# Three DRAM-to-DRAM weight sums of a hybrid encoder layer at other places of the weight plan

## The chip, the cores and the metric

The kernel runs on one core of a Trainium2 chip. The metric is the device time of one execution in microseconds; the time given for a kernel is the median of its runs. A profile is one further execution, taken with the hardware profiler; its times count from the first instruction.

## What is computed

One layer over 512 tokens of width 1024: an S5 state-space branch and a gated-MLP branch are merged by gates, then comes attention to 256 memory tokens, then a SwiGLU feed-forward with an inner width of 2816. Cut to what matters here:

```python
def memory_cross_attention(hn, memn, w_q, w_k, w_v, w_o):
    q = (hn @ w_q).reshape(bsz, seq, XATTN_HEADS, XATTN_HEAD_DIM)
    k = (memn @ w_k).reshape(bsz, MEM_LEN, XATTN_HEADS, XATTN_HEAD_DIM)
    v = (memn @ w_v).reshape(bsz, MEM_LEN, XATTN_HEADS, XATTN_HEAD_DIM)
    ...
    return o @ w_o

def swiglu(hn, w_gate, w_up, w_down):
    return (jax.nn.silu(hn @ w_gate) * (hn @ w_up)) @ w_down

        h = h + memory_cross_attention(rms_norm(h, xattn_norm_g[i]), memn,
                                       w_q[i], w_k[i], w_v[i], w_xo[i])
        h = h + swiglu(rms_norm(h, ffn_norm_g[i]), w_gate[i], w_up[i], w_down[i])
```

## The kernel before

**Split products.** Every float32 operand is split into a rounded high half (`whi`, a cast on ScalarE, line 85) and the rest (`wlo`, a subtraction on VectorE, line 86). A product takes three matmuls: high by high, high by low, low by high (`mm3`, line 358).

**Seven products for eight.** The products with w_proj_b, w_q, w_gate, w_up and w_down are made by a Strassen-Winograd scheme: of each 2 x 2 split of the weights, seven products instead of eight, four of which (numbers 4 to 7) need sums of weight blocks. For w_proj_b, w_q and w_down these sums are made in DRAM, ahead of time, by transfers alone. For w_down the results are `dsum4` to `dsum7`, each cut into six chunks of 512 KB, the last of 256 KB. Sum 5 and sum 7 add two blocks of w_down; sum 6 adds a block to sum 5, sum 4 a block to sum 6.

**The plan.** All weights are listed once, in the order of their use, in `plan`: 218 entries, each one block of at most 512 KB. An entry has a list of loads and a function that makes its two halves. `next_w` (called where TensorE's program takes entry i) starts the loads that are due by then and makes the halves up to two entries ahead. A load into SBUF is due three entries ahead (`LOADS`) and has three buffers (`wraw`), so the load of an entry waits until the halves of the entry three before are made; the two kinds of halves have three buffers each too.

The entries around the change: 64 to 71 are w_k, 72 to 79 are w_v (two halves of four blocks, two token tiles each, so 12 matmuls for a block), 80 to 93 the fourteen products with w_q (six blocks of w_q itself and eight of its sums, `qsum`), 94 to 101 w_xo, and 102 to 107 the first blocks of w_gate and w_up: 102 and 104 are the last 256 gate columns, 103 and 105 the first two blocks of the first gate unit, 106 and 107 the last 256 up columns. From 108 on come the units of the feed-forward, seven products each, and at the end w_down.

**The sums' places.** `plan_sums` makes a list of 40 jobs, in this order: sixteen for w_proj_b and w_q, then six chunks each of `dsum5`, `dsum7`, `dsum6` and `dsum4`. A job is two transfers: a plain copy of the first block from DRAM to DRAM, issued by SP (line 274), and an accumulating copy that adds the second block to it, issued by POOL (GpSimd, line 275). Job number m gets the m-th place (j, step): its copy is issued when entry j is taken, its accumulation when entry j + step is taken. The accumulation waits for the copy's landing.

**Queues.** SP issues nearly all loads, in order, so that a waiting load holds up those behind it. POOL issues the accumulations, in order too, and computes the norm factors (`r`, line 497), which a row's scaling (`xs`, line 512, VectorE) and its transposes (`ptr`, line 520, TensorE) wait for. The order on each engine is fixed when the program is built, by a scheduler with a model of time; a few instructions, the plain copies of the sums among them, are kept in the program's order.

Of the kernel before, what the change touches and what calls it, by code (L numbers as in the profile page):

```python
# [52 lines left out]
def hybrid_layer_kernel(  # L53
# [203 lines left out]
    def plan_sums(places):  # L257


        jobs = []  # L260
        pairs = {5: ((0, 0), (0, 1)), 7: ((0, 1), (1, 1)), 6: (None, (1, 1)), 4: (None, (1, 0))}
        for w, sums, qs in ((w_proj_b, bsum, (5, 7, 6)), (w_q, qsum, (5,)), (w_proj_b, bsum, (4,)), (w_q, qsum, (7, 6, 4))):
            for q in qs:
                first, more = pairs[q]
                for n in range(2):
                    jobs.append((sums[q, n], sums[q + (-1 if q == 6 else 2), n] if first is None else
                                 pair_block(w, *first, n), pair_block(w, *more, n)))
        for q, i, jc, more in ((5, 0, 0, lambda c: down_block(0, 1, c)), (7, 0, 1, lambda c: down_block(1, 1, c)),
                               (6, 1, 1, lambda c: down_sum(5, c)), (4, 1, 0, lambda c: down_sum(6, c))):
            for c in range(CHUNKS):  # L270
                jobs.append((down_sum(q, c), down_block(i, jc, c), more(c)))
        assert len(jobs) == len(places)
        for (dst, src, more), (j, step) in zip(jobs, places):
            plan[j][1].append((0, lambda d=dst, x=src: tc.keep_in_program_order(nc.sync.dma_start(d, x))))
            plan[j + step][1].append((0, lambda d=dst, x=more: nc.gpsimd.dma_start(d, x, accum_op=ALU.add)))
# [41 lines left out]
    for i in range(4):  # L317
# [5 lines left out]
    plan_units(UNITS, down_plan)  # L323

    plan_sums([(5, 3), (7, 3), (9, 2), (13, 5), (14, 5), (16, 4)] + [(18 + 2 * i, 3) for i in range(8)] +
              [(51 + 2 * i, 2) for i in range(4)] + [(85 + 3 * i, 3) for i in range(3)] +
              [(95 + 2 * i, 2) for i in range(3)] + [(122 + 4 * i, 4) for i in range(16)])
    used_w = [0]

    def next_w(*key):  # L330
# [1515 lines left out]
```

## Time and profile before

| | |
|---|---|
| median of 3 runs | 881.05 us (880.0 to 881.38) |
| profiled execution | 883.48 us |
| its span, first to last instruction | 881.7 us |
| mean granted TensorE clock | 0.992 |
| copies into `dsum` by SP | 24 (20 of 512 KB, 4 of 256 KB) |
| accumulations into `dsum` by POOL | 24 |

How it is read: the page gives busy times by engine and the chain of waits that ended last; the windows give busy times and the share of the DMA engines in a stretch of the span; a row of the timeline has its start, its length, engine and line, what it writes from what, and in brackets how long the engine was idle before it and what ended that. A DMA's row on SP or POOL is its issue, not its transfer; the time to landing is listed with the DMA issues.

### The profile page before, as it was taken

Reading aid. Unit: us, or ns where it says so; the run is one execution under the profiler, and the core shown is the slowest. Engines: PE = TensorE matmul, PEld = TensorE weight load, DVE = VectorE, ACT = ScalarE, POOL = GpSimd, SP = SyncE. Lnnn points to the kernel's source line nnn. Section 1 sums busy time; section 2 is a strip of 40 time slices with the busy share of each in tenths; the row PEclk is TensorE's granted clock in tenths of the full one; section 3 lists DMA queues with packets and bytes.
Section 4 is the critical chain, followed back from the end, with each engine's and each line's share of the span. In section 5 each row is a group of like instructions: output and inputs, shape, how many; then the busy total and the mean of one; then the engine's idle time right before and its main releaser. Section 6 shows DMA issues by size and latency. Waiting matters only on the chain.

```text
span 881.7 us, 14747 instructions
## 1 busy us (share of the span) xinstructions
PE 863.3 (98%) x5760; PEld 769.7 (87%) x5760; DVE 658.4 (75%) x1068; ACT 467.2 (53%) x692; POOL 86.4 (10%) x117
## 2 busy tenths in 40 slices
PE   8999999999998999999999999999999999999996
PEld 5788888888888988889899878999999999988875
DVE  5699885899845777658856836767878767899875
ACT  5643953244366553547555535645455455656664
POOL 1001301311000001100001001101211111000010
PEclk8999999999999999999999999999999999999999
DMA  7769565898664798735679645647999998366672
GB/s 239 197 191 298 104 179 148 183 234 193 166 195 115 241 285 258 245 112 156 207 218 256 172 108 159 168 123 168 228 232 236 211 239 215 96 187 207 193 237 96
DMA packets 117256, 169.56 MB, mean 192 GB/s; under 512 B 9265, under 2 KB 82497, under 8 KB 117058
## 3 DMA queue, kind: packets, MB, share of 16 engines
q1 hardware_dynamic: 97602, 141.64, 50.6%
q0 software_dynamic: 19296, 26.45, 19.2%
q8 instruction: 45, 0.74, 0.3%
q10 hardware_dynamic: 288, 0.52, 0.2%
q14 instruction: 25, 0.20, 0.1%
HBM read 159.71 MB, written 48.73 MB: 236 GB/s over the span
## 4 chain that ended last, share of the span: by engine, by line
PE 91%; DMA 4%; ACT 2%; DVE 2%; SPq 1%; issue 1%; POOL 0%; POOLq 0%; ACTq 0%; DVEq 0%
PE pf L358 26%; PE pt L358 17%; PE px L1146 12%; PE pq L1146 6%; PE dx L358 5%; PE dq L358 3%; PE pv L1146 3%; PE bx L1146 2%; PE qx L1146 2%; PE dv L358 2%; PE pz L889 2%; PE ptr L520 1%; PE po L358 1%; PE qv L1146 1%; DMA slab<-in_s_log_step_dram 1%; DMA wraw<-qsum 1%
## 5 line engine op out<-in xcount | busy, mean ns | idle before, releaser
L85 ACT CAST whi<-wraw 128x1024 fp32r<-128x1024 f32 (+1 forms) x145 | 148.6, 1025 | 158.0 <-PE pf L358 48.6
L86 DVE TENSOR_TENSOR wlo<-wraw,whi 128x1024 fp32r<-128x1024 f32 (+1 forms) x145 | 171.9, 1188 | 69.1 <-ACT whi L85 67.4
L358 PE MATMUL pf<-xn,whi 128*128 128x512 f32 x448 | 140.4, 393 | 0.0
L358 PEld LDWEIGHTS pf<-xn,whi 128*128 128x128 f32 x448 | 83.7, 188 | 17.5 <-issue 0.4
L358 PE MATMUL pf<-xn,wlo 128*128 128x512 f32 x224 | 87.8, 392 | 0.0
L1146 PE MATMUL px<-fn,whi 128*128 128x256 f32 x480 | 83.3, 276 | 0.0
L1146 PEld LDWEIGHTS px<-fn,whi 128*128 128x128 f32 x480 | 72.6, 188 | 0.2
L86 DVE TENSOR_TENSOR wlo<-b,whi 128x1024 fp32r<-128x1024 f32 x40 | 48.9, 1222 | 27.9 <-ACT whi L85 27.9
L85 ACT CAST whi<-b 128x1024 fp32r<-128x1024 f32 x40 | 42.2, 1054 | 50.8 <-PE px L1146 27.8
L1146 PE MATMUL px<-fn,wlo 128*128 128x256 f32 x240 | 66.4, 277 | 0.0
L1146 PE MATMUL pq<-s,whi 128*128 128x256 f32 x320 | 55.0, 276 | 0.0
L358 PE MATMUL dx<-whi,s 128*128 128x512 f32 x170 | 53.4, 391 | 0.4 <-DVE h L1771 0.4
L86 DVE TENSOR_TENSOR wlo<-t,whi 128x1024 fp32r<-128x1024 f32 x30 | 36.7, 1224 | 19.4 <-ACT whi L85 19.4
L85 ACT CAST whi<-t 128x1024 fp32r<-128x1024 f32 x30 | 31.6, 1053 | 35.3 <-PE pv L1146 12.4
L358 PEld LDWEIGHTS pf<-xn,wlo 128*128 128x128 f32 x224 | 42.1, 188 | 8.7 <-issue 0.2
L1146 PEld LDWEIGHTS pq<-s,whi 128*128 128x128 f32 x320 | 48.2, 188 | 0.0
L358 PE MATMUL pt<-whi,xn 128*128 128x512 f32 x128 | 44.6, 415 | 1.6 <-ACT xn L85 1.4
L1146 PEld LDWEIGHTS px<-fn,wlo 128*128 128x128 f32 x240 | 45.1, 188 | 0.0
L1146 PE MATMUL pq<-s,wlo 128*128 128x256 f32 x160 | 44.2, 276 | 0.0
L358 PEld LDWEIGHTS dx<-whi,s 128*128 128x128 f32 x170 | 31.8, 188 | 7.5 <-issue 0.8
L358 PE MATMUL dx<-wlo,s 128*128 128x512 f32 x85 | 33.1, 391 | 0.3 <-DVE wlo L86 0.3
L358 PEld LDWEIGHTS pt<-whi,xn 128*128 128x128 f32 x128 | 24.7, 195 | 7.8 <-ACT xn L85 2.0
(451 smaller groups left out, 2200.7 us busy)
## 6 DMA issues: line engine op xcount, KB each, us to landing
wraw<-in_w_in_dram SPq DMA_DIRECT2D x36, 512.0 KB, 4.6
dsum<-in_w_down_dram SPq DMA_DIRECT2D x20, 512.0 KB, 5.7
wraw<-dsum SPq DMA_DIRECT2D x20, 512.0 KB, 3.8
b<-in_w_gate_dram SPq DMA_DIRECT2D x15, 512.0 KB, 6.6
b<-in_w_up_dram SPq DMA_DIRECT2D x15, 512.0 KB, 5.6
wraw<-in_w_down_dram SPq DMA_DIRECT2D x15, 512.0 KB, 4.5
dsum<-in_w_down_dram POOLq DMA_DIRECT2D x10, 512.0 KB, 7.8
dsum<-dsum POOLq DMA_DIRECT2D x10, 512.0 KB, 7.6
```

The costliest lines, as they stand in the source:

```text
L85: hi = nc.scalar.copy(dst_hi, src)
L86: lo = nc.vector.tensor_tensor(dst_lo, src, dst_hi.bitcast(F32), ALU.subtract)
L358: m = nc.tensor.matmul(ps, a[x], b[y], start=start and i == 0, stop=stop and i == 2, skip_group_check=free)
L520: nc.tensor.transpose(ps[:, j, :], src[:, k * P:(k + 1) * P], ident)
L889: nc.tensor.matmul(ps[:, g, :], wt[:, g, :], u[:, o * GO + g, :], start=True, stop=True)
L1146: nc.tensor.matmul(ps[:, j, :], a[x], b[y], start=start and j == k == i == 0, stop=k == 3 and i == 2, skip_group_check=True)
```

## The change

Only the list of places changes. The three places 85, 88 and 91 among w_q's entries go; 73 and 76 among w_v's entries come, and 105 among the first gate and up blocks. Since jobs take the places in order, the jobs after them slide:

| job | before | after |
|---|---|---|
| 18: sum 5, chunk 2 | entry 85, added at 88 | 73, added at 76 |
| 19: sum 5, chunk 3 | 88, 91 | 76, 79 |
| 20: sum 5, chunk 4 | 91, 94 | 95, 97 |
| 21: sum 5, chunk 5 (256 KB) | 95, 97 | 97, 99 |
| 22: sum 7, chunk 0 | 97, 99 | 99, 101 |
| 23: sum 7, chunk 1 | 99, 101 | 105, 108 |

```diff
     plan_sums([(5, 3), (7, 3), (9, 2), (13, 5), (14, 5), (16, 4)] + [(18 + 2 * i, 3) for i in range(8)] +
-              [(51 + 2 * i, 2) for i in range(4)] + [(85 + 3 * i, 3) for i in range(3)] +
-              [(95 + 2 * i, 2) for i in range(3)] + [(122 + 4 * i, 4) for i in range(16)])
+              [(51 + 2 * i, 2) for i in range(4)] + [(73, 3), (76, 3)] +
+              [(95 + 2 * i, 2) for i in range(3)] + [(105, 3)] + [(122 + 4 * i, 4) for i in range(16)])
```

In the built program SP's copy of job 18 stands between w_v's fourth and fifth load, that of job 19 between its seventh and eighth, that of job 23 behind the second `wraw` load of w_up and ahead of the first unit's up blocks. On POOL the accumulation of job 23 stands between the third and the fourth norm factor of the feed-forward's norm. The other engines have the same instructions in the same order.

## The prediction

> **What bounds the kernel now.** I read the page first: its span, the busy times and the shares of the chain that ended last.
>
> ```profile
> span 881.7 us, 14747 instructions
> PE 863.3 (98%) x5760; PEld 769.7 (87%) x5760; DVE 658.4 (75%) x1068; ACT 467.2 (53%) x692; POOL 86.4 (10%) x117
> PE 91%; DMA 4%; ACT 2%; DVE 2%; SPq 1%; issue 1%; POOL 0%; POOLq 0%; ACTq 0%; DVEq 0%
> ```
>
> TensorE is busy for 863.3 of 881.7 us, so a change in transfers is worth only the TensorE idle time that it removes or adds. Then came the chain of waits over w_q's products, where the three sums stood:
>
> ```profile
> 459.84 9.48 DMA wraw<-qsum
> ...
> 471.78 2.39 PE qq L1146 x18
> ```
>
> The chain shows a load of 9.48 us, but a step of a chain is not a loss: TensorE was working most of that time. The loss is TensorE's idle time, in the windows (stretch and its length, busy us and count of PE, PEld, DVE, ACT and POOL, the clock, the share of DMA, GB/s) and in the waits:
>
> ```profile
> 468.00:472.00 4.00, 3.62 (x32) 3.42 (x31) 1.50 (x2) 2.58 (x4) 1.14 (x1) 1.00 1.01 296
> sum 42.00, PE 41.40 PEld 40.36 DVE 27.87 ACT 25.50 POOL 4.31; mean PE 0.49 PEld 0.48 DVE 0.33 ACT 0.30 POOL 0.05
> PE qq L1146 <- DVE wlo L86: 0.4, 1, 0.4
> PE ppt L1432 <- DVE prob L1423: 0.2, 1, 0.2
> ```
>
> The sum is over 84 windows of half a microsecond from 449 to 491, the whole stretch after the first of the three copies: TensorE is idle for 42.00 - 41.40 = 0.60 us in all. Of that the late weights cost 4.00 - 3.62 = 0.38 us, once; the other 0.22 is the wait of the transposes (ppt) for the softmax, which holds no weight load.
>
> **The change, part by part.** TensorE, ScalarE and VectorE keep every instruction and its order; only the places of plain copies (SP, line 274) and accumulating copies (POOL, line 275) move. Jobs 18 and 19 (third and fourth chunk of sum 5) go from w_q's entries 85 and 88 to w_v's 73 and 76. The next four jobs slide one place down the list of places: 91, 95, 97, 99 become 95, 97, 99, 105. So entry 91 is freed and 105 is new. No copy and no byte is added: 24 copies and 24 accumulations stay.
>
> *Removed from w_q's products:* three copies and three accumulations. Beside them two loads took 7.3 and 9.5 us, where the median of w_v's (below) is 3.7 (DMA issues, each from a window with that issue alone, issued at 457.12 and 459.84):
>
> ```profile
> wraw<-qsum SPq DMA_DIRECT2D x1, 512.0 KB, 7.3
> wraw<-qsum SPq DMA_DIRECT2D x1, 512.0 KB, 9.5
> 455.68 1.18 POOL L275 DMA_DIRECT2D dsum<-in_w_down_dram  x1 [54.58 <-DMA dsum<-in_w_down_dram]
> 457.51 0.56 SPq L274 DMA_DIRECT2D dsum<-in_w_down_dram  x1
> 468.65 1.14 POOL L275 DMA_DIRECT2D dsum<-in_w_down_dram  x1 [11.79 <-DMA dsum<-in_w_down_dram]
> ```
>
> Worth: -0.38 us. Upper bound -0.60, if the softmax's 0.22 goes as well; lower bound 0, if the loads stay late. I take -0.4. What is late next there is the softmax's wait.
>
> *Added among w_v's products.* What does one job cost the DMA engines? The quietest one is the copy at 515.08 with its accumulation at 520.12:
>
> ```profile
> 514.66 0.37 SPq L137 DMA_DIRECT2D wraw<-in_w_xo_dram  x1
> 515.08 0.56 SPq L274 DMA_DIRECT2D dsum<-in_w_down_dram  x1
> 520.12 1.14 POOL L275 DMA_DIRECT2D dsum<-in_w_down_dram  x1 [22.62 <-DMA dsum<-in_w_down_dram]
> 522.00:525.50 3.50, 3.50 (x17) 2.75 (x16) 1.92 (x2) 1.64 (x2) 0.00 (x0) 1.00 1.01 149
> ```
>
> The copy, 0.4 us behind a load, lands 5.0 us after its issue. The accumulation starts moving 1.9 us after POOL begins to issue it and then fills the 16 engines (share 1.01) for 3.5 us. Now the value stage:
>
> ```profile
> 416.89 0.37 SPq L137 DMA_DIRECT2D wraw<-in_w_v_dram  x1
> 421.76 0.37 SPq L137 DMA_DIRECT2D wraw<-in_w_v_dram  x1
> 424.37 0.37 SPq L137 DMA_DIRECT2D wraw<-in_w_v_dram  x1
> 426.97 0.37 SPq L137 DMA_DIRECT2D wraw<-in_w_v_dram  x1
> 429.24 0.37 SPq L137 DMA_DIRECT2D wraw<-in_w_v_dram  x1
> wraw<-in_w_v_dram SPq DMA_DIRECT2D x1, 512.0 KB, 5.2
> wraw<-in_w_v_dram SPq DMA_DIRECT2D x8, 512.0 KB, 3.7
> 419.01 21.97 PE pt L358 x96
> 425.43 1.05 ACT L85 CAST whi<-wraw 128x1024 fp32r<-128x1024 f32 x1 [1.13 <-DMA wraw<-in_w_v_dram]
> 429.70 1.05 ACT L85 CAST whi<-wraw 128x1024 fp32r<-128x1024 f32 x1 [3.23 <-DMA wraw<-in_w_v_dram]
> 430.79 1.23 DVE L86 TENSOR_TENSOR wlo<-wraw,whi 128x1024 fp32r<-128x1024 f32 x1 [1.58 <-ACT whi L85]
> 433.13 2.35 DVE L86 TENSOR_TENSOR wlo<-wraw,whi 128x1024 fp32r<-128x1024 f32 x2
> ```
>
> The five loads are w_v's fourth to eighth; the 5.2 us is the sixth's. The 96 products run 21.97/96 = 0.229 us apart, 12 to a block. By the order of PE's instructions the fifth block's hi half is first read by product 37 (419.01 + 36 x 0.229 = 427.25), the sixth's lo half by product 63 (433.2), the eighth's by product 87 (438.7). The fifth's hi half is ready at 425.43 + 1.05 = 426.48, the sixth's lo at 430.79 + 1.23 = 432.02, the eighth's at 433.13 + 2.35 = 435.48. So the slack is 0.8, 1.2 and 3.2 us. Two of these three casts already wait for their load. w_q's first block follows the last of the 96, at 441; I give its loads the eighth's 3 us.
>
> The first copy goes out right behind the fourth load, at 417.3, and lands at about 422.3. Its accumulation then moves data from 422.3 + 1.9 = 424.2 to about 427.7: on top of the sixth load, issued at 424.37. Sharing turns, the load loses up to half of 3.5 us, 1.75; less the slack of 1.2 that is a stall of 0.6. The fifth load, issued before, loses about 0.5, within its 0.8. The second copy stands at 427.4, ahead of the eighth load; that load comes later by the copy's own data, an estimate of 1.75 us (half an accumulation's 3.5, as it reads one block where that reads two), and by the 1.75 still owed: 3.5 against 3.2, 0.3. The second accumulation (about 435 on) meets w_q's first loads, with their 3 us: 0. Sum taken: +0.9. Bounds: 0, if every load stays within its slack; and the lateness seen in w_q, 9.5 - 3.7 = 5.8 less 1.2 = 4.6 us for the first job and 5.8 - 3.2 = 2.6 for the second, 7.2 in all. I take a value near the lower end, because the job is alone here whereas the 9.5 had a copy and an accumulation of two jobs around it.
>
> *Issue slots.* A copy takes SP 0.56 to 0.70 us; SP has nothing to issue from 417.3 to 421.76 nor from 427.4 to 429.24, so this is hidden by SP's own waiting for buffers (without that cover, 0.6 each). On POOL only other accumulations stand behind these two.
>
> *w_xo.* Its first copy now moves a whole chunk where it moved half a one, its second half a one where it moved a whole one, and its third, at 515.08, as much as before.
>
> ```profile
> 482.23 0.54 SPq L274 DMA_DIRECT2D dsum<-in_w_down_dram  x1
> 484.00:488.00 4.00, 4.00 (x32) 3.83 (x32) 3.03 (x6) 3.42 (x8) 0.46 (x1) 1.00 0.49 179
> ```
>
> Behind the first the engines have room (share 0.49), so 0; without that room it is half of the accumulation's 3.5 us and half of a copy's 1.75, some 2.6.
>
> *The third sum, at the gate.* Its copy follows the second w_up load on SP, its accumulation the third of four norm factors on POOL, and the fourth factor now stands behind it:
>
> ```profile
> 550.10 0.37 SPq L137 DMA_DIRECT2D wraw<-in_w_up_dram  x1
> 557.68 0.55 POOL L497 TENSOR_TENSOR r<-ms,mhalf 128x1 f32<-128x1 f32 x1 [4.52 <-DVE ms L496]
> 558.27 1.41 DVE L512 SCALAR_TENSOR_TENSOR xs<-h,r,g_f 128x512 f32<-128x512 f32 x2
> 561.57 0.60 PE L520 MATMUL ptr<-ident,xs 128*128 128x128 f32 x4
> 548.00:552.00 4.00, 4.00 (x24) 3.31 (x23) 2.42 (x3) 3.02 (x7) 0.00 (x0) 1.00 0.19 24
> 572.00:584.00 12.00, 12.00 (x108) 12.00 (x108) 9.00 (x9) 5.59 (x6) 0.00 (x0) 1.00 0.01 1
> ```
>
> Copy at 550.5, landed at 550.5 + 5.0 = 555.5 on nearly idle engines (0.19), accumulation issued until 556.7: 1.0 us before the factor is wanted. Behind it wait xs on VectorE and the last token tile's transposes, which run at 561.57, 1.9 us after xs ends (558.27 + 1.41): 2.9 us in all until TensorE stalls. Its 5 us of transfers delay the up unit's loads, but the engines are idle from 572 to 584. I take 0. Upper bound: a copy as slow as the one issued at 457.51, whose accumulation started 11.1 later, at 468.65, makes the factor 5 us late and TensorE 3.2.
>
> Sum: -0.4 + 0.9 + 0 = +0.5. The profiled execution took 883.48 us (1.8 around its span), so 884.0; the median of the three runs shown is 881.05, 2.4 lower, and there the same difference gives 881.5.
>
> **The rivals.** *Slower through w_v's loads.* The sixth load lands more than 1.2 us late (after about 430.8): the accumulation, whose 3.5 us of data fall on it, takes the engines nearly whole. For it speaks that the load issued 1.4 us after the accumulation of 455.68 took 7.3, which is 3.6 late, and the one behind the second copy 9.5, which is 5.8 late. Less 1.2 that is a stall of 2.4 to 4.6; the eighth load then has 3.2 + 2.4 = 5.6 us and adds 0.2 at most. With -0.4: +2.0 to +4.2, its middle +3.1, 884.1. Against it: no second copy stands right behind this load.
>
> By the Trainium skill (DMA: Bandwidth & Descriptors, section "Queues, rings and completion order") each DMA engine takes turns between the queues that have work, a packet at a time. By that rule a load beside an accumulation is late by up to the accumulation's whole data, an estimate of 3.5 us, and the sum would be +1.9 from the first job alone; the 7.3 us load agrees with it.
>
> *Slower through POOL.* The fourth norm factor waits for the third sum's copy. It decides from a landing after 558.4; priced at 3.2 - 0.4 = +2.8, 883.9. Against it: the engines' share of 0.19 there.
>
> *Faster by more than 0.2%.* It needs 1.8 us, and the stage's whole idle time is 0.60. It could only come if unprofiled executions lose more in w_q than this profile: about 879.
>
> *The change does nothing:* the late loads move along with the sums and cost the same 0.4 in w_v. 881.05, within the forecast's own band.
>
> **How the numbers follow.** What this kernel's measurement can tell from no change is about 0.2%, 1.8 us. Forecast with the rival that nothing happens: 0.55, 880.4 to 882.8. Slower through w_v's loads 0.33, through POOL 0.05: 0.38. Faster 0.07. The range for 8 in 10 leaves out most of the faster case and the top of the slower one: 879.8 to 884.8. The predicted time is the likeliest case's, 881.5.
>
> **What would show it.** Right: w_q's loads back at 3 to 5 us, no TensorE idle at 471; in w_v the sixth load at 6 to 7.5 us and TensorE idle for 0.3 to 1 us between 427 and 440; no idle before the transposes of the fourth token tile. Wrong: windows of w_v with TensorE idle for 2 us or more, a wait of PE for wlo at the start of w_q, or transposes waiting for the fourth factor.

## The result, and the profile after

The changed kernel takes 883.24 us (median of 22 runs, 879.93 to 889.0), the kernel before 879.67 beside it (22 runs, 877.88 to 883.25): a ratio of 1.0036, with a 95% interval of 1.0023 to 1.0048. By the ratio that is 3.2 us slower, 2.0 to 4.2 (the two medians are 3.6 us apart). The forecast had 881.5, the range 879.8 to 884.8.

The two profiled executions hide this: 883.48 us before, which is more than any of its 22 runs, and 883.89 after. The page of after has the same work on every engine:

```profile
span 882.1 us, 14748 instructions
PE 863.6 (98%) x5760; PEld 767.8 (87%) x5760; DVE 658.4 (75%) x1068; ACT 467.2 (53%) x692; POOL 86.5 (10%) x117
```

So I compared by stage. The groups of the tile `bx` (the state-space branch; the change begins behind it) and of `po` (the first product behind w_q's, with w_xo) give the last start of the one and the first of the other. Behind the count stand the least, median and most ns of one, then the first and last start. Before:

```profile
L1146 PE MATMUL bx<-yb_hi,wlo x48: 276/281/281, 271.9 to 312.1; 128*128 128x256 f32 x48
L358 PE MATMUL po<-p_hi,vt x32: 388/391/478, 486.9 to 525.8; 128*128 128x512 f32 x32
```

And after:

```profile
L1146 PE MATMUL bx<-yb_hi,wlo x48: 276/276/280, 270.2 to 309.8; 128*128 128x256 f32 x48
L358 PE MATMUL po<-p_hi,vt x32: 388/393/478, 487.0 to 525.9; 128*128 128x512 f32 x32
```

After reached the end of `bx` 2.3 us sooner, where no instruction differs: from 280 to 284 the granted clock was 0.58 in the profile of before, which loses 1.7 us, and 1.00 in that of after. By `po` the lead was gone. One window from the one point to the other, its length first and TensorE's busy time behind the comma, gives the stage of before:

```profile
312.10:486.90 174.80, 174.19 (x1093) 156.44 (x1093) 122.96 (x169) 93.74 (x148) 11.68 (x15) 1.00 0.73 217
```

and of after:

```profile
309.80:487.00 177.20, 175.44 (x1092) 157.02 (x1091) 123.30 (x169) 93.58 (x148) 10.55 (x14) 0.99 0.68 210
```

The stage is 2.4 us longer: 1.76 us idle where there were 0.61, and busy 1.25 us longer for the same matmuls. Where? The chain of waits of after, in w_v's second half (start, length, what; pieces of under 0.05 us are left out):

```profile
421.95 8.41 DMA wraw<-in_w_v_dram
...
430.47 1.05 ACT whi L85
...
431.54 1.24 DVE wlo L86
...
432.82 9.66 PE pt L358 x34
```

The sixth load of w_v takes 8.41 us, where it took 5.2 before. What moved beside it, from the timeline (start, length; the brackets give the engine's idle time and what ended it):

```profile
414.90 0.56 SPq L274 DMA_DIRECT2D dsum<-in_w_down_dram  x1
420.34 1.18 POOL L275 DMA_DIRECT2D dsum<-in_w_down_dram  x1 [21.65 <-DMA dsum<-in_w_down_dram]
433.47 1.14 POOL L275 DMA_DIRECT2D dsum<-in_w_down_dram  x1 [11.95 <-DMA dsum<-in_w_down_dram]
```

Job 18's copy lands 5.4 us after its issue and its accumulation goes out at once, 1.6 us ahead of the sixth load. (Before the prediction it is said that an accumulation is issued when entry j + step is taken. That is its place in POOL's program; POOL runs ahead of the other engines, so in time the copy's landing decides.) The waits of TensorE there, and the windows of 2 us (busy PE, PEld, DVE, ACT, POOL, then granted clock, DMA share, GB/s):

```profile
PE pt L358 <- ACT whi L85: 1.2, 1, 1.2
PE pt L358 <- DVE wlo L86: 0.5, 1, 0.5
```

```profile
428.00:430.00 2.00, 2.00 (x11) 1.57 (x9) 0.00 (x0) 0.00 (x0) 0.00 (x0) 1.00 1.03 378
430.00:432.00 2.00, 0.77 (x4) 0.30 (x2) 0.46 (x1) 1.53 (x3) 0.00 (x0) 1.00 0.91 350
432.00:434.00 2.00, 1.48 (x6) 0.97 (x5) 2.00 (x4) 1.43 (x2) 0.53 (x1) 0.84 0.23 85
434.00:436.00 2.00, 2.00 (x7) 1.54 (x6) 1.70 (x2) 1.04 (x1) 0.61 (x1) 0.50 1.00 265
436.00:438.00 2.00, 2.00 (x9) 1.62 (x8) 0.63 (x1) 0.99 (x1) 0.00 (x0) 0.81 0.98 148
```

TensorE is idle for 1.23 + 0.52 = 1.75 us, and behind that the granted clock is 0.84, 0.50 and 0.81 for 2 us each: 2 x (0.16 + 0.50 + 0.19) = 1.7 us of clock are lost although TensorE reads as busy. In w_q's products TensorE now has no idle time from 444 to 490, and the loads of w_q's sums take 4.1 us as a median, where the median of before in that stretch was 5.3 and its worst two took 7.3 and 9.5:

```profile
wraw<-qsum SPq DMA_DIRECT2D x6, 512.0 KB, 4.1
```

The third sum, at the gate, on POOL:

```profile
555.71 1.18 POOL L275 DMA_DIRECT2D dsum<-in_w_down_dram  x1 [2.48 <-DMA dsum<-in_w_down_dram]
557.76 0.56 POOL L497 TENSOR_TENSOR r<-ms,mhalf 128x1 f32<-128x1 f32 x1 [0.88 <-DVE ms L496]
```

The fourth norm factor still waits for its input `ms` and comes 0.08 us later in the span than before; the whole stretch already stood 0.1 us later at `po`. In this profile the third sum costs nothing.

### The profile page after: what moved, and what is told of

Same layout as the page of the kernel before. It is cut to its first block, busy times and chain, and to the rows that moved or that the text cites. A ratio compares the mean times of both kernels' runs of the same rounds, so it can differ in the third digit from the quotient of the medians.

```text
span 882.1 us, 14748 instructions
## 1 busy us (share of the span) xinstructions
PE 863.6 (98%) x5760; PEld 767.8 (87%) x5760; DVE 658.4 (75%) x1068; ACT 467.2 (53%) x692; POOL 86.5 (10%) x117
## 4 chain that ended last, share of the span: by engine, by line
PE 86%; DMA 6%; DVE 3%; ACT 2%; issue 1%; SPq 1%; POOL 0%; POOLq 0%; ACTq 0%; DVEq 0%
PE pf L358 23%; PE pt L358 16%; PE px L1146 12%; PE pq L1146 6%; PE dx L358 5%; PE dq L358 3%; PE pv L1146 3%; PE qx L1146 2%; PE dv L358 2%; PE bx L1146 2%; PE pz L889 1%; DVE wlo L86 1%; PE psc L358 1%; PE qq L1146 1%; PE ptr L520 1%; PE po L358 1%
## 5 line engine op out<-in xcount | busy, mean ns | idle before, releaser
L1146 PEld LDWEIGHTS pq<-s,wlo 128*128 128x128 f32 x160 | 30.1, 188 | 0.0
```

The costliest lines, as they stand in the source:

```text
L1146: nc.tensor.matmul(ps[:, j, :], a[x], b[y], start=start and j == k == i == 0, stop=k == 3 and i == 2, skip_group_check=True)
```

## The experiments

The main theory: the loss is one load of w_v, made late by job 18's accumulation. Rivals: the two plain copies on SP, the third sum, or the slide of the jobs behind. Twelve more runs were made; e8, e11 and e12 repeat a kernel. Except where its diff shows more, each has only another list of places. In the table, "stage" is the window from the last `bx` product to the first `po` product; "extra busy" is TensorE's busy time there less the 173.20 of the quietest execution (for e7 it holds 1.55 us of added matmuls).

| kernel | sums at w_v, w_q, gate | stage, us | idle | extra busy | ratio (95%) |
|---|---|---|---|---|---|
| before | 0, 3, 0 | 174.8 | 0.61 | 0.99 | |
| e12 before again | 0, 3, 0 | 173.2 | 0.00 | 0.00 | 1.0016 (0.9998 to 1.0034) |
| after | 2, 0, 1 | 177.2 | 1.76 | 2.24 | 1.0036 (1.0023 to 1.0048) |
| e8 after again | 2, 0, 1 | 176.4 | 2.23 | 0.97 | 1.0043 (1.0023 to 1.0063) |
| e1 | 2, 1, 0 | 176.9 | 1.42 | 2.28 | 1.0033 (1.0017 to 1.0048) |
| e2 | 0, 2, 1 | 173.4 | 0.00 | 0.20 | 0.9990 (0.9973 to 1.0007) |
| e11, as e2 | 0, 2, 1 | 174.4 | 0.33 | 0.87 | 1.0000 (0.9985 to 1.0015) |
| e3 | 2 copies only, 0, 1 | 173.4 | 0.00 | 0.20 | 0.9989 (0.9968 to 1.0009) |
| e4 | 0, 0, 3 | 173.5 | 0.00 | 0.30 | 0.9998 (0.9980 to 1.0015) |
| e5 | 2 accumulations alone, later | 174.1 | 0.43 | 0.47 | 1.0007 (0.9992 to 1.0023) |
| e6 | 1, 1, 1 | 176.0 | 1.98 | 0.82 | 1.0021 (1.0003 to 1.0038) |
| e7 | as after, filled | 176.4 | 0.72 | 2.48 | 1.0031 (1.0010 to 1.0052) |
| e9 | 2 accumulations alone, sooner | 174.9 | 1.29 | 0.41 | 1.0022 (1.0005 to 1.0039) |
| e10 | 2, an entry later | 177.9 | 2.34 | 2.36 | 1.0059 (1.0041 to 1.0076) |

### Each part alone (e1, e2, e4)

```diff
 e1_wv_two
-[(73, 3), (76, 3)] + [(95 + 2 * i, 2) for i in range(3)] + [(105, 3)]
+[(73, 3), (76, 3), (91, 3), (95, 2), (97, 2), (99, 2)]
 e2_gate_one
+[(85, 3), (88, 3), (95, 2), (97, 2), (99, 2), (105, 3)]
 e4_quiet
+[(95, 2), (97, 2), (99, 2), (106, 2), (107, 2), (108, 2)]
```

> Only the two sums beside w_v (73, 76); the other four jobs keep their old places (91, 95, 97, 99). Theory W (w_v's late loads cost it all: TensorE waits and then a lower granted clock): 2.5 to 4 us over the kernel before, TensorE idle for 1 to 3 us between 425 and 440 and a clock below 1.0 in some windows behind it. Rival G (the third sum at the gate, or the slide of the later jobs, costs it): within 1 us of before.

> Only the slide: 85 and 88 stay in w_q, the later four jobs go to 95, 97, 99, 105. Theory W: within 1 us of before, or up to 0.6 faster, as w_q loses one job of three. Rival G: 2.5 to 4 us slower.

> No job beside w_v or w_q: six jobs at 95, 97, 99, 106, 107, 108, where the DMA engines have idle stretches (572 to 584). Theory W: no wait in either stage, 0.3 to 1 us faster than before. Rival G (jobs behind w_xo and at the gate cost time): slower than before by 1 us or more.

The two sums at w_v alone bring a loss as large as the change's (884.42 against 880.33 us, ratio 1.0033), and without the fall of the clock that was expected with it: the granted clock is 1.00 in every window of w_v and w_q. The third sum alone, with the slide it forces (880.06), and all three at the gate (880.41) can't be told from before. So the loss sits in w_v. In the five profiles without a job there (before, e12, e2, e11, e4) the sixth load took 4.7 to 5.3 us; in the five with job 18 at its new place (after, e8, e1, e6, e7) it took 8.0 to 8.6.

### The copies without the accumulations (e3)

The accumulations of jobs 18 and 19 are left out, so that part of `dsum5` stays without its second block.

```diff
-            plan[j + step][1].append((0, lambda d=dst, x=more: nc.gpsimd.dma_start(d, x, accum_op=ALU.add)))
+            if j not in (73, 76):
+                plan[j + step][1].append((0, lambda d=dst, x=more: nc.gpsimd.dma_start(d, x, accum_op=ALU.add)))
```

> The changed kernel without the accumulations of the jobs at 73 and 76 (two adds into the third and fourth chunk of sum 5 are left out); their plain copies stay beside w_v's loads. Theory W with the accumulations as the cause: no wait of TensorE in w_v above 0.3 us, time 0.3 to 1 us below the kernel before, since w_q is relieved as well. Rival C (the plain copies in SP's queue ahead of the eighth load delay it): TensorE still waits 1 us or more in w_v, 2 to 4 us slower than before.

879.51 us, ratio 0.9989. The sixth load's issue and the cast that waits for it, in the timeline of e3:

```profile
422.77 0.37 SPq L137 DMA_DIRECT2D wraw<-in_w_v_dram  x1
428.05 1.05 ACT L85 CAST whi<-wraw 128x1024 fp32r<-128x1024 f32 x1 [3.20 <-DMA wraw<-in_w_v_dram]
```

5.3 us from issue to cast, as before (424.37 to 429.70), with both copies in place. All that shows of the copies is at the eighth load, issued 1.9 us behind the second of them: it took 5.2 us, and 3.5 to 4.0 in the five profiles without a job there. That is within its lead, and TensorE doesn't wait. The accumulations do the harm.

### Only the first sum at w_v (e6)

```diff
+[(73, 3), (88, 3), (95, 2), (97, 2), (99, 2), (105, 3)]
```

> The first early sum alone stays beside w_v's weights; the second goes to the gate's weights with the third (their copies then stand 17 us apart). Theory (the first sum's accumulation, which runs while the sixth load does, is enough): sixth load over 7 us, TensorE idle over 1 us before its products, 1.5 to 4.0 us slower than before. Rival (it takes the second sum's copy beside it): sixth load under 7 us, idle time under 0.5 us, within 0.8 us of before.

The expectation misnames the second sum's place: it stands at 88, among w_q's entries, as one of before's did. The time is 881.09, ratio 1.0021. The accumulation goes out at 418.86, and the sixth load has this row in the chain of e6:

```profile
420.51 8.62 DMA wraw<-in_w_v_dram
```

The stage has 1.98 us of idle time. Job 18 alone makes the wait; job 19, whose accumulation (433.47 in after) starts behind the eighth load, is not needed for it.

### The accumulations at other moments (e5, e9, e10)

In e5 and e9 the whole copies of jobs 18 and 19 are taken some 50 us sooner, and a copy of 8 partitions, repeated, holds the accumulation's place among the loads.

```diff
 e5_wv_adds, e9_add_sooner
+            if j in (73, 76):
+                at = 60 if j == 73 else 62
+                plan[at][1].append((0, lambda d=dst, x=src: tc.keep_in_program_order(nc.sync.dma_start(d, x))))
 ... (the other jobs keep their copy, in an else branch)
 e5_wv_adds
+                plan[j + 1][1].append((0, lambda d=dst[0:8], x=src[0:8]: tc.keep_in_program_order(nc.sync.dma_start(d, x))))
 e9_add_sooner
+                plan[j][1].append((0, lambda d=dst[0:8], x=src[0:8]: tc.keep_in_program_order(nc.sync.dma_start(d, x))))
 e10_later, from the changed kernel
-[(73, 3), (76, 3)]
+[(74, 3), (77, 3)]
```

> The changed kernel with the plain copies of its two early sums done some 40 us sooner (in the stretch before, where w_xo is multiplied), so that only the two accumulations, 512 KB each, fall among w_v's loads; a copy of 8 of their 128 partitions is repeated at the old places, so that the accumulations start when they did. Theory (the accumulations delay w_v's sixth load): that load still takes over 7 us, TensorE idles 1 to 2 us before the sixth block's products, 2.0 to 4.0 us slower than before. Rival (copy and accumulation are needed together): the load lands within 6 us, no idle time over 0.3 us there, within 0.8 us of before.

> As the run with the copies taken ahead, but the small copies of 8 partitions stand one entry sooner, so that the first accumulation starts 1 to 3 us sooner against w_v's loads than in the changed kernel, where that run had it 3 us later. Theory (it takes the copy and the accumulation, each of which sets the loads back by 1 to 3 us, to use up the lead that the loads have): no wait on TensorE over 0.3 us between 425 and 440, within 1.2 us of before. Rival (the accumulation alone does it, where it starts ahead of the sixth load): sixth load over 7 us, idle time over 1 us, 1.5 to 4 us slower than before.

> The changed kernel with both early sums one entry later (74 and 77): w_v's fifth load goes out ahead of the first copy, the eighth ahead of the second. Theory (the loads' whole delay counts, wherever the sum stands among them): a load of w_v over 6.5 us, the sixth or the seventh, TensorE idle 0.5 to 1.8 us before its products, 1 to 3.5 us slower than before. Rival (it is the sixth load alone, by where the first accumulation meets it): idle time under 0.3 us between 425 and 442, within 1 us of before.

The accumulation's issue, the next load of w_v and the cast that waits for it. For e9 the load is in the chain of waits:

```profile
418.03 6.04 DMA wraw<-in_w_v_dram
```

```profile
417.25 1.18 POOL L280 DMA_DIRECT2D dsum<-in_w_down_dram  x1 [19.88 <-issue]
424.16 1.04 ACT L85 CAST whi<-wraw 128x1024 fp32r<-128x1024 f32 x1 [3.61 <-DMA wraw<-in_w_v_dram]
```

For e5:

```profile
426.73 1.18 POOL L280 DMA_DIRECT2D dsum<-in_w_down_dram  x1 [24.75 <-DMA dsum<-in_w_down_dram]
427.85 0.37 SPq L137 DMA_DIRECT2D wraw<-in_w_v_dram  x1
434.26 1.05 ACT L85 CAST whi<-wraw 128x1024 fp32r<-128x1024 f32 x1 [2.23 <-DMA wraw<-in_w_v_dram]
```

For e10:

```profile
427.53 1.18 POOL L275 DMA_DIRECT2D dsum<-in_w_down_dram  x1 [26.44 <-DMA dsum<-in_w_down_dram]
429.23 0.37 SPq L137 DMA_DIRECT2D wraw<-in_w_v_dram  x1
438.93 1.04 ACT L85 CAST whi<-wraw 128x1024 fp32r<-128x1024 f32 x1 [6.41 <-DMA wraw<-in_w_v_dram]
```

Each time the load issued 0.8 to 1.7 us behind the accumulation is late: the fifth in e9 (6.0 us), the sixth in after (8.4), the seventh in e5 (6.4), the eighth in e10 (9.6). The loads behind it are late as well (the sixth of e9 took 7.2 us, the seventh and eighth of after 7.1 and 7.4), but have more lead. Whether TensorE waits depends on the lead of the late load. The seventh had enough (e5: no wait in w_v, and 1.0007); the fifth and the eighth had not (1.29 us of idle time in e9, 2.34 in e10, the most expensive run).

So e5's theory fell: its accumulation came one load later than it was meant to, and no wait followed. e9's theory, that it takes the copy too, fell, and its rival stood: the accumulation makes TensorE wait without its whole copy beside it, though for the fifth load and not for the sixth. e10's theory had the mechanism right; it was wrong in naming the sixth or the seventh load, and too low in the idle time (0.5 to 1.8 us) and in the price: 1.0059 is 5.2 us, from six runs. Its profile has a fall of the clock behind the wait, as that of after had:

```profile
440.00:442.00 2.00, 1.44 (x5) 0.93 (x6) 1.23 (x1) 0.49 (x1) 1.14 (x1) 0.98 0.22 88
442.00:444.00 2.00, 2.00 (x7) 1.52 (x6) 1.38 (x2) 1.79 (x3) 0.00 (x0) 0.50 0.86 184
444.00:446.00 2.00, 2.00 (x11) 1.71 (x10) 1.67 (x2) 0.85 (x2) 0.00 (x0) 0.67 1.09 223
```

Where the whole copy had been done long before (e9, e5), the late load took 6.0 and 6.4 us; where it had only just landed (after, e6, e10), 8.4, 8.6 and 9.6. Two things differ at once between them, the moment and the copy, so what makes this difference isn't shown. Job 19's copy isn't needed for it, since e6 has none in w_v.

### Both kernels again, and the wait filled (e8, e12, e7)

```diff
 e7_fill6, in the changed kernel
+    def fill():
+        t = aux("idle")
+        for i in range(FILL):
+            in_order(nc.tensor.matmul(t, mn_hi[:, 0, 0:P], mn_hi[:, 0:2, :], start=True, stop=True))
+    FILL = 6
-        tokm(w_v, half * 512, mn, KD, v_evac(half), ntok=NM)
+        tokm(w_v, half * 512, mn, KD, v_evac(half), ntok=NM, hooks={1: fill} if half else {})
```

> The changed kernel with 6 matmuls more (their results aren't used) ahead of the products of w_v's sixth block in the second half, about 1.7 us of TensorE's time by the mean of the products there (0.28 us), which would be its wait otherwise. Theory (the wait costs about twice its length, since the granted clock falls to between 0.5 and 0.84 for 6 us behind it): the clock stays above 0.95 from 428 to 442, 1.0 to 2.0 us faster than the changed kernel, 1.2 to 2.2 us slower than before. Rival (the fall of the clock costs nothing, or doesn't hang on the wait): within 0.6 us of the changed kernel.

> The changed kernel itself, as the measure for the three runs beside it. Theory: 2.3 to 4.0 us slower than before, TensorE idle 1.2 to 2.0 us between 430 and 436, with a fall of the granted clock below 0.9 behind it. Rival (the fall of the clock in the first profile was a chance of that execution): the same idle time, clock above 0.95 throughout.

e8 measured 883.36 us, ratio 1.0043, and its second profile has the same load late (8.13 us), TensorE idle there for 0.95 + 0.52 = 1.47 us, and no fall of the clock:

```profile
428.00:430.00 2.00, 1.05 (x5) 0.53 (x5) 0.15 (x1) 1.23 (x2) 0.00 (x0) 1.00 1.05 409
430.00:432.00 2.00, 1.48 (x6) 0.90 (x7) 2.00 (x3) 1.74 (x3) 0.19 (x1) 1.00 0.47 182
432.00:434.00 2.00, 2.00 (x10) 1.63 (x9) 1.68 (x3) 1.05 (x1) 0.95 (x1) 1.00 0.90 252
```

So the rival was right: the fall of the clock is a chance of the execution, and TensorE waits without it. That it isn't what sets the median is borne out by the mean granted clock of the runs, 0.9964 over the 22 of after and 0.9962 over e8's 12, beside 0.9958 over the 35 of before that belong to e8: a loss of 1.7 us in each run would lower it by 0.0019. The profile of e8 has instead a second wait of 0.8 us, at w_q's second load (its first of a sum), which is issued 1.6 us behind job 19's accumulation (at 431.81) and takes 7.33 us in the chain of e8:

```profile
433.43 7.33 DMA wraw<-qsum
```

The filler of e7 did fill the wait (430.89, six matmuls in 1.55 us; 0.58 us of idle time is left in w_v), and the clock stayed at 1.00; but it stayed there in e8 as well. 882.58 us against 883.36, with intervals that overlap: e7 decides nothing on the clock's price.

> The kernel before itself, for a second profile of the stretch that the stage times are measured against (the last two expectations' words on where the second and third sums stand were wrong: the run named for one sum at the gate keeps the other two at w_q's weights, 85 and 88, and the run with the first sum alone keeps the second at 88). Theory (w_q's late loads cost the kernel before a wait in every execution): TensorE idles 0.3 to 1.0 us between 455 and 485, and 174.2 to 175.4 us lie between the last bx product and the first po product. Rival (whether a load meets an accumulation hangs on the execution): no wait there, 173.2 to 173.8 us. The time within 0.1% of before.

The kernel before, run as if it were a change, came out at 1.0016, more than the 0.1% expected: two groups of runs of one kernel can differ by 1.3 us. Its second profile has no idle time from `bx` to `po`:

```profile
310.30:483.50 173.20, 173.20 (x1092) 155.90 (x1091) 123.46 (x169) 93.90 (x148) 11.68 (x15) 1.00 0.72 220
```

The theory of that run fell. Its rows at w_q, beside those of before in the prediction (accumulation at 455.68, loads issued at 457.12 and 459.84):

```profile
453.30 1.18 POOL L275 DMA_DIRECT2D dsum<-in_w_down_dram  x1 [54.18 <-DMA dsum<-in_w_down_dram]
462.92 1.05 ACT L85 CAST whi<-wraw 128x1024 fp32r<-128x1024 f32 x1 [2.56 <-DMA wraw<-qsum]
465.50 1.05 ACT L85 CAST whi<-wraw 128x1024 fp32r<-128x1024 f32 x1 [1.05 <-DMA wraw<-qsum]
```

The second late load, issued at 457.86, lands by 465.50, 7.6 us where it took 9.48, and its cast waits 1.05 us where it waited 3.41. That is early enough for TensorE. The wait at w_q that the change was priced to remove is there in one of the two profiles of before.

### The third sum's move once more (e11)

The kernel is that of e2.

> The kernel with all three sums at the gate's weights once more, for a second measure of what moving them away from w_q brings where it costs nothing. Theory (w_q's relief is worth what its stage shows): 0.6 to 1.8 us faster than before, and 168.5 to 173.6 us from the end of the bx products to the first po product is 1.0 to 1.8 us shorter than before's. Rival (the stage's gain is given back later): within 0.4 us of before.

This expectation, too, misnames the kernel: one sum is at the gate, and two stay at w_q. The two measures of it are 0.9990 and 1.0000, so the theory of 0.6 to 1.8 us gained isn't borne out and the rival stands; the two stages are 173.4 and 174.4 us long. In the longer one a load of a q sum takes 9.21 us, issued 4.1 us behind an accumulation, and TensorE idles 0.33 us: the wait of before, again in one of two profiles. No version that ran beats the kernel before beyond its interval.

## Why the prediction was right or wrong

*What bounds the kernel:* right. No experiment moved the time beyond its interval without moving TensorE's idle time or its pace.

*Removed from w_q's products, -0.4:* right in place, wrong in how firm it is. In the profiled pair it was worth more: the w_q stretch (first `qx` product, 440.8 before and 442.3 after, to first `po` product) shrank from 46.1 to 44.7 us, -1.4: 0.61 of idle time, and 0.79 in which TensorE was busy longer for the same products. But the second profile of before has no such wait, so the gain is a chance between 0 and some 1.4 us. The bounds (0 to -0.60) took idle time for the whole price.

*Added among w_v's products, +0.9:* the term that was mis-sized. The place, the sixth load, its lo half and its slack of 1.2 us were right; the step that failed is "Sharing turns, the load loses up to half of 3.5 us, 1.75". The load went from 5.2 to 8.4 us, 3.2 late: nearly the whole of the accumulation's 3.5 us of data. Less the slack of 1.2 that makes 2.0, and 1.75 of idle time were measured (1.47 in e8, 1.98 in e6). The price then grows by what the prediction had no term for, TensorE being busy longer for the same products. In all, the stretch from the last `bx` to the first `qx` product grew from 128.7 to 132.5 us: +3.8 where 0.9 was taken, of which 1.75 are idle time and 1.7 the clock of that execution; in e8, without the fall of the clock, it took 130.6 us. Over the whole stage the extra busy time of the runs with a wait in w_v is 0.4 to 2.4 us (e7 with its added matmuls left aside). The two profiles of each kernel put the stage of after 1.6 to 4.0 us above that of before; how the 3.2 us of the medians divide into idle time and pace isn't settled closer than that. The reason given for the low value, that the job is alone here, didn't hold: e6 has it alone, and the load is as late (8.6 us).

By the Trainium skill (DMA: Bandwidth & Descriptors, section "Queues, rings and completion order") the engines take turns between the queues that have work. The prediction estimated from it a load late by up to an accumulation's whole data, 3.5 us, and a sum of +1.9. The late load of after agrees with that, 3.2 us against 3.5; the eighth load of e10 doesn't, which took 9.6 us where it takes 3.5 to 4.0 without a job there.

*The eighth load and w_q's first loads, +0.3 and 0:* the eighth load was as late as predicted (7.4 us where it took 3.7 before; 3.5 late were taken), but made no wait, as TensorE itself came later by then. w_q's loads made none in the first profile and 0.8 us in e8, so 0 was a little low.

*Issue slots and w_xo, 0:* right. From the first to the last `po` product pass 38.9 us in both kernels.

*The third sum, 0:* right. From the last `po` product to the first of `pv` (the feed-forward's gate and up products) pass 37.8 us before and 37.9 after, and e2 with it alone costs nothing. The rival "slower through POOL" has no trace.

*The cases:* 3.2 us slower is not the forecast's +0.5 but the rival "slower through w_v's loads", +2.0 to +4.2 with a middle of +3.1. It was listed with its mechanism, its price and a chance of 0.33. Its estimate came from the loads beside the accumulations in w_q, which were 3.6 and 5.8 us late, and this nearest measured case was better than the model of half shares that was preferred to it. So the range held the result because it took in most of this rival, and not because the sum was right: the sum had +0.5 of 3.2. That the rival's middle comes so close is in part luck, too, since its stall of 2.4 to 4.6 us was 1.75 and 1.47, and the pace, for which it had no term, made up for it. Of the signs named beforehand, the sixth load (8.4 us, not 6 to 7.5) and the idle time (1.75, not 0.3 to 1) lie outside the right case, and the wait for `wlo` at the start of w_q, named as a sign of being wrong, came in e8.

## What to carry to other kernels

Price a transfer on a busy queue by a load that already runs beside such a transfer in the same trace, not by a share worked out for it. Here an accumulation from DRAM to DRAM delayed the load issued just behind it by 3.2 us, nearly all of its own data time of 3.5, and by 2.4 to some 6 us at other places; TensorE waits for that delay less the lead of that very load, and the whole cost was more than the wait. Weigh the wait that is removed in more than one execution: this one was in one of two profiles, while the late load it was traded for was in all five profiles that had a whole sum at that place. Run the unchanged kernel as a change once: 1.0016 here tells how far 0.2% can be trusted.

## What had not been expected

**A short wait can halve the clock behind it, and need not.** 1.75 us of idle time in after were followed by the fall to 0.50 shown above, and 2.34 us in e10 by a like one: each lost 1.7 us of clock. 1.29 us in e9, 1.37 in e1, 1.47 in e8 and 1.98 in e6 weren't. The Trainium skill (TensorE: Matmul & The Clock Gate, section "What's actually happening") has the clock halve after an idle window of about 3.4 us that runs freely. The level, half, and the chance agree with the trace; the length doesn't, since a wait of half a window was enough.

**TensorE can be slower at full clock, too.** In e1 the products behind the wait take 4% longer for over 30 us, at a granted clock of 1.00 in every window there. In the chains 24 products of e1 take

```profile
464.71 2.83 PE qx L1146 x24
```

and of after

```profile
462.93 2.72 PE qx L1146 x24
```

In before, too, the products behind the wait at w_q are slow for a while:

```profile
474.17 2.84 PE qx L1146 x24
```

But e8 and e6, with waits as long or longer, are at 2.72 us there, and the same step shows in the rows of `bx` above, a median of 281 ns before and 276 after, without any change. So it isn't shown that the wait brings it, and what sets it was not found.
